# Narrow loads of the third tile: 768 columns instead of 1024, dealt anew over the DMA engines

## The chip, the cores and the metric

The kernel runs on one core of a Trainium2 chip. The metric is the device time of one execution in microseconds. The kernel before takes 2485.12 us (median of 3 runs, 2485.06 to 2485.26).

## The reference

A softmax with a temperature over the last axis of 16 x 256 rows of 32768 float32 numbers; the temperature is 1.0.

```python
scaled = logits / temperature
scaled = scaled - scaled.max(axis=-1, keepdims=True)
exp_scaled = np.exp(scaled)
return (exp_scaled / exp_scaled.sum(axis=-1, keepdims=True)).astype(np.float32)
```

512 MiB are read and 512 MiB written, and each number is read once and written once.

## The kernel before, in words

Each row of 32768 numbers is cut into two halves of 16384, so that the input is a matrix of 8192 half rows. 64 tiles of 128 half rows (8 MiB each) go one after the other through three slots of one large buffer in on-chip memory: tile g uses slot g modulo 3. Both halves of a row lie on neighbouring partitions of the same tile.

For each tile VectorE takes the maximum of three pieces of the half rows (L217), ScalarE makes the exponentials in place with the piece's own maximum and sums them (L277), and a few small instructions on both engines exchange the maxima and sums of neighbouring partitions and make one factor per piece (L235 to L262). ScalarE then scales the first piece (L296) and VectorE the two others (L268). The last two tiles have six smaller pieces. The instructions of VectorE and ScalarE stand in order: four tiles, a loop over three slots with 19 turns, and three tiles.

All transfers are issued by SyncE, in the order that `order` (L94) writes out by hand: loads of tiles 0, 1 and 2, store of tile 0, load of 3, stores of 1 and 2, and then load i, store i - 1 up to the end. A load (`load`, L137) waits until the store of the tile that was in its slot three tiles ago has landed (L145); a store (`store`, L156) waits until the tile is scaled (L162, L166). A plain load or store is one transfer of 128 rows of 64 KB, eight rows on each of the 16 DMA engines. Tile 0 is stored and tile 3 loaded in two halves, and the last tile is stored in three parts.

Tile 2 (`_SPLIT`) is the exception that the change is about. `load_parts` (L80) cuts it in a wide part and a narrow part of `_NARROW` columns at the end of the rows. The wide part is one transfer of 128 rows (L154). The narrow part is loaded in 19 transfers, each with the few rows of one list that `narrow_rows` (L69) makes from `_NARROW_ROWS`, the longest list first (L148 to L151):

```python
if g == _SPLIT and j == 1:
    for some in narrow_rows(P):
        sig.dma(
            key, nc.sync.dma_start(out=X[some, where], in_=x[rows, s : s + n][some])
        )
else:
    sig.dma(key, nc.sync.dma_start(out=X[:, where], in_=x[rows, s : s + n]))
```

A list of n rows takes every ninth row from its first one on. In the trace such a transfer of n rows puts one row on each of n DMA engines, the same first ones each time. So the lists set how many narrow rows each engine moves. The consumer waits for the wide part before its first piece and for all 19 narrow transfers before the piece that reaches into their columns (`landed`, L201).

Of the kernel before, what the change touches and what calls it, by code (L numbers as in the profile page):

```python
# [11 lines left out]
_LATE = ((4096, 3072, 3072, 2048, 2048, 2048), (3, 4, 5))  # L12
_LAST_STORES = ((0, 4096), (4096, 6144), (10240, 6144))
_SPLIT = 2
_NARROW = 1024
_NARROW_ROWS = (
    (13, 2), (12, 3), (14,), (11, 3), (10, 4), (9, 5), (8, 6), (7, 7), (4, 4, 3, 3),
)
_HEAD = 4
_TAIL = 3  # L20
# [329 lines left out]
```

## Time and profile before

| | before |
|---|---|
| median of 3 runs | 2485.12 us (2485.06 to 2485.26) |
| the profiled execution's own time | 2485.08 us |
| its span, first to last instruction | 2483.3 us |
| VectorE busy | 1526.0 us, 61% |
| ScalarE busy | 1325.5 us, 53% |
| DMA packets' time on the SyncE queue, share of 16 engines | 99.9% |
| data moved | 1073.78 MB, 432 GB/s over the span |

The span ends with SyncE's last wait for the stores. Between the span and the execution's time lie 1.8 us of launch and exit. The DMA share of a stretch counts a packet where it starts. The trace also keeps the start, the duration and the size of each DMA packet, but not on which of the 16 engines it ran.

### The profile page before, as it was taken

What the parts mean: (1) busy time and instruction counts of PE and PEld (TensorE: products, weight loads), DVE (VectorE), ACT (ScalarE), POOL (GpSimd) and SP (SyncE); (2) the same over time, 40 slices, a digit from 0 to 9 for tenths busy, and PEclk for the clock granted to TensorE, in tenths of its full rate; (3) what the DMA queues carried; (4) which work ended last, traced back from release to release, by engine and by line L of the source; (5) the groups of instructions that cost most, each with busy time, mean ns of one, the idle gap of its engine ahead of it and who ended that gap; (6) DMA issues with size and microseconds to landing.
All of it is one profiled execution on the core that took longest, in us unless ns stands there. A gap on an engine that the chain in (4) does not pass through costs nothing.

```text
span 2483.3 us, 1689 instructions
## 1 busy us (share of the span) xinstructions
DVE 1526.0 (61%) x776; ACT 1325.5 (53%) x529; POOL 0.2 (0%) x4
## 2 busy tenths in 40 slices
DVE  5845665666656656566565665656656666566665
ACT  4744654646546455464554645546455464554654
POOL 0000000000000000000000000000000000000000
DMA  9999999999999999999999999999999999999999
GB/s 409 438 433 438 431 432 438 432 435 432 434 436 429 436 436 433 432 438 433 430 436 435 434 434 435 437 429 437 435 432 434 437 436 430 436 436 431 435 436 391
DMA packets 19267, 1073.78 MB, mean 432 GB/s; under 512 B 2240, under 2 KB 2240, under 8 KB 2368
## 3 DMA queue, kind: packets, MB, share of 16 engines
q1 hardware_dynamic: 19264, 1073.75, 99.9%
q14 instruction: 3, 0.02, 0.0%
HBM read 536.87 MB, written 536.87 MB: 432 GB/s over the span
## 4 chain that ended last, share of the span: by engine, by line
DMA 61%; DVE 28%; ACT 7%; issue 2%; SPq 0%; DVEq 0%
DMA xs<-in_logits_dram 59%; DVE t L217 21%; ACT xs L277 6%; DVE xs L268 6%; DMA out_dram<-xs 3%; SPq L171 0%; ACT ee L288 0%; DVE junk L262 0%; DVE t L235 0%; ACT xs L296 0%; DVE row L259 0%; DVE row L239 0%; DVE junk L246 0%; DVEq L309 0%; DVEq L233 0%
## 5 line engine op out<-in xcount | busy, mean ns | idle before, releaser
L277 ACT ACTIVATE xs<-xs,t 128x6304 f32<-128x6304 f32 (+5 forms) x198 | 932.0, 4707 | 1052.1 <-DVE t L217 1045.3
L217 DVE TENSOR_REDUCE t<-xs 128x1 f32<-128x6304 f32 (+5 forms) x198 | 1110.0, 5662 | 617.0 <-DMA xs<-in_logits_dram 617.0
L296 ACT ACTIVATE xs<-xs,junk 128x6304 f32<-128x6304 f32 (+1 forms) x68 | 355.6, 5235 | 44.9 <-DVE junk L262 44.9
L268 DVE TENSOR_SCALAR xs<-xs,junk 128x5376 f32<-128x5376 f32 (+2 forms) x130 | 358.7, 2802 | 2.3
L235 DVE LOAD_MASK_SELECT t<-t x64 | 0.9, 14 | 282.9 <-ACT xs L277 282.9
L288 ACT ACTIVATE ee<-t,row 128x6 f32<-128x6 f32 (+1 forms) x64 | 19.2, 300 | 35.2 <-DVE row L239 35.2
L277 ACT ACTIVATION_READ_ACCUMULATOR xs<-xs,t 128x1 f32 x198 | 36.9, 186 | 0.0
L246 DVE CUSTOM_DVE_ANT_1 junk<-ee,t 128x6 f32<-128x6 f32 (+1 forms) x64 | 10.7, 167 | 23.5 <-ACT ee L288 23.5
L262 DVE TENSOR_SCALAR junk<-ee,row 128x3 f32<-128x3 f32 (+1 forms) x64 | 14.6, 228 | 2.2
L259 DVE RECIPROCAL row<-row 128x1 f32<-128x1 f32 x64 | 10.4, 163 | 2.2
L239 DVE TENSOR_REDUCE row<-t 128x1 f32<-128x6 f32 (+1 forms) x64 | 10.2, 159 | 2.2
L235 DVE STREAM_SHUFFLE t<-t 128x6 f32<-128x6 f32 (+1 forms) x64 | 10.4, 163 | 0.5
L246 DVE DVE_READ_ACCUMULATOR2_ANT row<- 128x1 f32 x64 | 5.3, 83 | 0.0
L277 ACT ACT_TABLE_LOAD x1 | 1.3, 1283 | 0.9 <-SPq L128 0.9
L331 POOL MEMSET const-bfloat16-1.0<- 128x1 bf16 x1 | 0.1, 102 | 0.0
L331 POOL MEMSET const-uint8-127<- 128x1 uint8 x1 | 0.1, 101 | 0.0
L331 POOL MEMSET const-float32-0.0<- 128x1 f32 x1 | 0.1, 99 | 0.2 <-issue 0.2
L331 POOL MEMSET const-float32-1.0<- 128x1 f32 x1 | 0.1, 98 | 0.0
## 6 DMA issues: line engine op xcount, KB each, us to landing
out_dram<-xs SPq DMA_DIRECT2D x2, 4096.0 KB, 26.9
xs<-in_logits_dram SPq DMA_DIRECT2D x2, 4096.0 KB, 19.4
xs<-in_logits_dram SPq DMA_DIRECT2D x1, 7680.0 KB, 59.7
out_dram<-xs SPq DMA_DIRECT2D x2, 3072.0 KB, 19.4
out_dram<-xs SPq DMA_DIRECT2D x1, 2048.0 KB, 12.2
xs<-in_logits_dram SPq DMA_DIRECT2D x62, 48.1
out_dram<-xs SPq DMA_DIRECT2D x62, 29.1
xs<-in_logits_dram SPq DMA_DIRECT2D x4, 12.0 KB
```

Of the source, the lines that this page charges most:

```text
L217: m = v.tensor_reduce(out=t[:, k : k + 1], in_=self.piece(k), axis=mybir.AxisListType.X, op=A.max, negate=True,)
L235: v.stream_shuffle(out=t[:, 2 * K : 4 * K], in_=t[:, 0 : 2 * K], mask=swap), "sh"
L239: v.tensor_reduce(out=r[:, 0:1], in_=tv[:, :, 0, :], axis=mybir.AxisListType.XY, op=A.min),
L246: v.tensor_tensor_reduce(out=f[:, 0 : 2 * K].rearrange("p (a k) -> p a k", a=2), in0=self.ev, in1=tv[:, :, 1, :], scale=1.0, scalar=0.0, o ...
L259: self.done(v.reciprocal(out=r[:, 2:3], in_=r[:, 1:2]), "rc")
L262: v.tensor_scalar_mul(out=f[:, 0:K], in0=e[:, 0:K], scalar1=r[:, 2:3]), "f"
L268: v.tensor_scalar_mul(out=xs, in0=xs, scalar1=f[:, k : k + 1]), k, self.p.own
L277: s = a.activation(out=xs, in_=xs, func=Exp, bias=t[:, k : k + 1], scale=inv_t, accum_out=t[:, K + k : K + k + 1],)
L288: a.activation(out=self.ev, in_=self.tv[:, :, 0, :], func=Exp, bias=r[:, 0:1], scale=-1.0),
L296: self.scaled(a.mul(out=xs, in_=xs, mul=f[:, k : k + 1]), k, self.p.on_act)
L331: nc = _bacc.Bacc("TRN2", target_bir_lowering=False, num_devices=1)
```

## The change

The narrow part of tile 2 becomes 768 columns wide instead of 1024, so the wide part grows from 15360 to 15616 columns, and the rows are dealt to other lists. There are 19 lists before and after.

```diff
-_NARROW = 1024
+_NARROW = 768
 _NARROW_ROWS = (
-    (13, 2), (12, 3), (14,), (11, 3), (10, 4), (9, 5), (8, 6), (7, 7), (4, 4, 3, 3),
+    (15,), (12, 3), (14,), (14,), (13, 1), (10, 4), (8, 6), (4, 4, 4, 2), (4, 4, 4, 2),
 )
```

Each group in round brackets deals the rows q, q + 9, q + 18 and so on of one remainder q, in order, to lists of the lengths given; one list has a single row after the change. On SyncE the 19 narrow transfers are issued from the same place, right behind the wide part's, and nothing else moves on any engine: the order of the instructions of VectorE, ScalarE and SyncE is the same but for the sizes of these 20 transfers.

## Prediction

> **What bounds the kernel now.** I read the page from the top: busy times, the DMA rows, the queue, and then the SyncE queue's timeline, because DMA came out as the bound.
>
> ```profile
> span 2483.3 us, 1689 instructions
> ...
> DVE 1526.0 (61%) x776; ACT 1325.5 (53%) x529; POOL 0.2 (0%) x4
> ...
> DMA  9999999999999999999999999999999999999999
> ...
> DMA packets 19267, 1073.78 MB, mean 432 GB/s; under 512 B 2240, under 2 KB 2240, under 8 KB 2368
> ...
> q1 hardware_dynamic: 19264, 1073.75, 99.9%
> ```
>
> VectorE has 39% of the span free and ScalarE 47%. The 16 DMA engines have nothing free: 99.9%. The chain of waits names VectorE and ScalarE too, but only because each store is issued after them; the engines meanwhile have other packets queued. The 2368 - 2240 = 128 packets between 2 and 8 KB are the narrow loads, one 4 KB packet per row.
>
> The trace keeps every packet's start, duration and size. An engine starts its next packet 3 to 4 ns before the modelled end of the last, so the packets can be threaded into 16 chains. I number the chains by how many 4 KB packets they hold: 19, 19, 18, 14, 11, 10, 9, 7, 6, 5, 4, 3, 2, 1, 0, 0. That is exactly "a transfer of n rows puts one row on each of the first n engines". No chain has a gap over 0.75 us, so an engine's last packet ends at its start plus its own work plus what its packets lose to contention. The slowest engine sets the end. The DMA share in stretches at the end shows how unequal they are:
>
> ```profile
> 2476.00:2476.50 0.50, 0.00 (x0) 0.00 (x0) 0.00 (x0) 1.00 0.69 295
> 2476.50:2477.50 1.00, 0.00 (x0) 0.00 (x0) 0.00 (x0) 1.00 0.68 295
> 2477.50:2479.00 1.50, 0.00 (x0) 0.00 (x0) 0.00 (x0) 1.00 0.53 229
> 2479.00:2480.50 1.50, 0.00 (x0) 0.00 (x0) 0.00 (x0) 1.00 0.19 82
> 2480.50:2482.00 1.50, 0.00 (x0) 0.00 (x0) 0.00 (x0) 1.00 0.04 16
> ```
>
> The last two columns are DMA share and GB/s. Engines drop out from 2476.0 on; engines 11 to 15 end at 2476.0 to 2476.3, engines 0 to 3 at 2480.6 to 2480.8, and engine 4 last of all at 2481.60 us. From there to the profiled time of 2485.08 us are 3.48 us of completion and exit, which I keep. The profiled run is 0.04 us under the median of 2485.12 us, so the sum holds for both.
>
> **The change, part by part.**
>
> Issue. The 19 narrow issues of SyncE stay 19.
>
> ```profile
> 0.95 1.32 SPq L154 DMA_DIRECT2D xs<-in_logits_dram  x3
> 2.31 13.89 SPq L151 DMA_DIRECT2D xs<-in_logits_dram  x19
> 51.70 0.84 SPq L171 DMA_DIRECT2D out_dram<-xs  x2
> ```
>
> They are done at 16.2 us; the engines reach them at about 58 us. Cost nothing, hidden by 42 us of queued tiles. Behind them waits only the first store, issued at 51.70 after ScalarE, not after them.
>
> Landing. Tile 2's reduce starts at 80.19 us and its last third, the only one that reads narrow columns, near 92 us, while the narrow packets end before 64 us. Cost nothing; cover 28 us.
>
> Work of each engine. Packets outside contention: 64 KB 2418 ns, 60 KB 2267, 32 KB 1213, 16 KB 611, 4 KB 159; so 37.65 ns per KB. The wide load's eight packets grow from 60 to 61 KB: +301 ns on every engine. A narrow packet shrinks to 3 KB, 121.4 ns; with its 9 ns completion packet and two overlaps of 3.6 ns, one narrow load costs an engine 161.2 ns before and 123.6 after. With the new counts (row lists read the same way) each engine's work changes by 301 + 123.6 x new - 161.2 x old:
>
> ```
> engine      0    1    2    3    4    5    6    7    8    9   10   11   12   13   14   15
> old count  19   19   18   14   11   10    9    7    6    5    4    3    2    1    0    0
> new count  19   18   16   15    8    8    7    7    6    6    5    5    4    3    1    0
> change ns -413 -537 -623 -102 -483 -322 -284  +38  +75 +237 +275 +435 +473 +511 +425 +301
> ```
>
> By this alone engine 4 ends at 2481.60 - 0.48 = 2481.12, engine 3 at 2480.66, and the time is 2481.12 + 3.48 = **2484.6 us**.
>
> What the Trainium skill says of a row list with one row in it. The trace of before has no one-row transfer; its smallest, two rows, went to two engines. "DMA: Bandwidth & Descriptors", section "Why a DMA increments its semaphore by 16 and not by 1", says the count of engines is the largest number up to 16 that divides the slowest dimension that is not 1; for one row that would be the 768 columns, so 16 packets of 192 B. By this rule engine 0 loses one 123.6 ns load and all engines gain a packet, an estimate of some 20 ns each by the rows' 9 ns completion packet; the sum would be 2484.6 still.
>
> Losses at the narrow loads themselves. Around 57 to 61 us the last wide packet took 0.2 to 1.2 us too long on 14 engines, and six of the 128 narrow ones 0.5 to 0.8 us instead of 0.16, where some engines are in their narrow loads and others still in the wide one; engine 0 stood 0.74 us. A narrow row need not go to the engine that writes its partition in a wide load, so two engines may be writing where one did. As many narrow loads start among the same wide packets after the change, with other partners. I take the same losses; bounds are none of them (about 1 us off every engine) and half as much again (0.5 us more).
>
> Contention later on. This is the term with most freedom, since the order in which engines run is what the change moves. In the trace almost every packet that is long after 64 us is the last of a load's eight: 113 of 123 that are over by 15 ns or more. An engine that is behind reads its last packet while those ahead already store, and loses 30 to 550 ns there. That pushes it further back, until it no longer meets them; from 1250 us on all engines but number 4 take 2418 ns a packet, with three or four exceptions. Lags behind the first engine, at its first store and at the end: engines 0 to 3 from 2.3-3.1 to 4.6-4.7 us; engines 5, 6 and 8 from 1.1-1.3 to 3.2-3.5; engines 7, 9 and 10 from 0.6-0.8 to 1.3-1.7; engines 11 to 15 stay under 0.45. Engine 4 goes from 1.57 to 5.56; of this 2.0 us are a trickle of its own, 0.2 us in each 250 us, to the end.
>
> After the change the lags at the first store are (old start plus change): engines 0 to 3 at 2.2, 2.1, 1.9 and 1.7 us, and twelve engines within 0.7 us, number 4 at 0.58. The first engine ends 0.5 us later, at 2476.55. Bounds: with no push, engines 0 to 3 end at 2476.55 + 2.2 = 2478.75 and engine 4 at 2476.55 + 0.58 + 2.0 = 2479.1, time 2482.6; with the old spread formed again, 2476.55 + 5.56 = 2482.1, time 2485.6. I take the old push for the four: 2.2 + 1.5 = 3.7, end 2480.25, time 2483.7. Engine 4 with the push of its new nearest neighbour by lag (old engine 10, 0.60 to 1.31: 0.7) ends at 2479.8, with its own old push of 4.0 at 2481.1, time 2484.6. Between 2483.7 and 2484.6, **2484.1 us**.
>
> A measurement of this kernel can tell about 0.2%, 5 us, from no change; so 2480.1 to 2490.1 counts as the same.
>
> **The rivals.**
>
> 1. *The old spread forms again* (slower than before, 0.5 us). Twelve engines in 0.7 us are a crowd where five stood; if no more than some five can stay together, the rest is pushed back group by group and drives engines 0 to 3 ahead of it. For it: the gaps of 0.8 to 1.6 us between the groups at the end of before. Against it: engines under 0.8 us behind lost next to nothing until 800 us. It decides where the pushes add up to over 3 us: 2485.6 us, up to 2487 with the engine-4 trickle falling on the last group.
> 2. *No push.* The twelve lie below the 0.8 us at which losses began, and engines 0 to 3 have only one group ahead of them, over 1 us clear. Against it: engine 4 was at 1.57 and was pushed. 2482.6 us.
> 3. *The losses do not die out* (slower). Place: the last packet of each load on engines 0 to 3, with twelve engines storing at once. Price: engine 8 lost 2.0 us from 200 to 1000 us, that is 97 ns at each of some 20.7 loads; over 62 loads 6.0 us, so 2478.75 + 6.0 + 3.48 = 2488.2; at its worst stretch (1.02 us from 600 to 800 us) 12 us, 2494. It passes "slower" from 130 ns a load on. Against it: in before every group came free by 1250 us. Beside it stands "DMA: Bandwidth & Descriptors", section "Latency and other measured facts", row on HBM row pitch: lock-stepped streams from rows a large power of two apart fell from 207 to 164 and 103 GB/s. Its pitches begin at 512 KiB and here rows lie 64 KiB apart; the trace speaks against a loss of that kind, since between 7.4 and 50 us all 16 engines ran within 1.1 us of each other and no 64 KB packet took over 2444 ns.
> 4. *It does not do what it says:* the trace has no one-row transfer, and the new one might be split over all 16 engines in place of one. Then engine 0 has one load of 123.6 ns less and every engine a small packet more, which by the 9 ns packets and the 37.65 ns per KB is some 25 ns with its completion. It moves no case by more than 0.15 us (3 in 10, inside the others).
>
> **How the numbers follow.** Forecast 2483 to 2485: 0.47. Rival 1, 2485 to 2487: 0.27. Rival 2, 2482 to 2483: 0.17. Rival 3: 0.08, half of it over 2490.1. Left, 0.01, for a gain over 0.2%: the mean of all 16 ends is 2478.5, which with perfect balance would give 2482.0, so only a loss of contention on top of that could do it. Range 2482.0 to 2487.0. Faster 0.01, same 0.95, slower 0.04.
>
> **What would show it.** Wide load 7808 KB, and 3 KB packets of some 121 ns: the work term. The DMA share falling from 2476.5 on instead of 2476.0, and one late group near 2480: the forecast; an engine ending at 2482: rival 1; all over by 2479.2: rival 2; long last packets still there past 1250 us: rival 3; packets under 512 B above 2240: rival 4. Wrong altogether if an engine runs dry: the tightest place is the last tile's first store, issued 1.29 us before the first engine starts it; a first engine later by 0.5 us only widens that.

## Result, and the profile after

The changed kernel takes 2507.82 us (median of 20 runs, 2485.31 to 2511.45), against 2485.15 us before (20 runs, 2484.68 to 2486.06). The ratio of the mean times is 1.0071, 95% interval 1.0053 to 1.009 (of the medians 1.0091): slower, and outside the forecast of 2482 to 2487 us. The runs of before lie within 1.4 us. Those of the changed kernel fall in two groups: four of 20 at 2485.3 to 2488.2 us, near the forecast, and sixteen at 2496.6 to 2511.5. The profiled one took 2496.59 us, with a span of 2494.8 us.

The page of the changed kernel, the lines that answer to those of before:

```profile
span 2494.8 us, 1689 instructions
...
DVE 1526.2 (61%) x776; ACT 1325.5 (53%) x529; POOL 0.2 (0%) x4
...
DMA  9999999999999999999999999999999999999998
...
DMA packets 19267, 1073.78 MB, mean 430 GB/s; under 512 B 2240, under 2 KB 2240, under 8 KB 2368
...
q1 hardware_dynamic: 19264, 1073.75, 99.8%
```

The same work, and still 99.8% of 16 engines busy: the page hardly shows the loss, because a packet that takes longer counts as busy for longer. That no packet under 512 B was added says that the one-row load was not split. The end, by stretches (last columns DMA share and GB/s):

```profile
2486.00:2487.00 1.00, 0.00 (x0) 0.00 (x0) 0.00 (x0) 1.00 0.41 172
2487.00:2488.50 1.50, 0.00 (x0) 0.00 (x0) 0.00 (x0) 1.00 0.27 115
2488.50:2490.00 1.50, 0.00 (x0) 0.00 (x0) 0.00 (x0) 1.00 0.30 131
2490.00:2491.50 1.50, 0.00 (x0) 0.00 (x0) 0.00 (x0) 1.00 0.30 131
2491.50:2493.50 2.00, 0.00 (x0) 0.00 (x0) 0.00 (x0) 1.00 0.09 37
```

From 2487 us on only some five engines of sixteen work. By the threaded packets eleven end at 2486.7 to 2486.9 us, one at 2490.6, and engines 0 to 3 at 2492.4 to 2493.2. So both moved: the first end by 10.7 us (2476.0 before) and the distance from first to last end from 5.6 to 6.5 us. The issues at the start are as they were:

```profile
0.96 1.33 SPq L154 DMA_DIRECT2D xs<-in_logits_dram  x3
2.33 13.24 SPq L151 DMA_DIRECT2D xs<-in_logits_dram  x19
51.63 0.85 SPq L171 DMA_DIRECT2D out_dram<-xs  x2
```

Where the time went is told by equal stretches of the middle, here of the changed kernel:

```profile
310.00:620.00 310.00, 190.73 (x96) 165.32 (x64) 0.00 (x0) 1.00 1.00 435
620.00:930.00 310.00, 190.73 (x96) 165.32 (x64) 0.00 (x0) 1.00 1.00 433
930.00:1240.00 310.00, 190.74 (x96) 165.31 (x64) 0.00 (x0) 1.00 1.00 434
1240.00:1550.00 310.00, 190.74 (x96) 165.31 (x64) 0.00 (x0) 1.00 1.00 435
1550.00:1860.00 310.00, 190.74 (x96) 165.33 (x64) 0.00 (x0) 1.00 1.00 433
1860.00:2170.00 310.00, 189.93 (x96) 164.58 (x64) 0.00 (x0) 1.00 1.00 427
```

Before has 433 to 435 GB/s in each of them, and in the last:

```profile
1860.00:2170.00 310.00, 190.70 (x96) 165.31 (x64) 0.00 (x0) 1.00 1.00 434
```

Until about 1800 us the kernel is nearly as fast as before: its store at 1778.86 us is 2.9 us later than the same one of before. Then it drops to 427 GB/s with 100% DMA share. SyncE's queue in that part, a store and the next load at each tile:

```profile
1974.50 0.33 SPq L171 DMA_DIRECT2D out_dram<-xs  x1
1974.87 0.43 SPq L154 DMA_DIRECT2D xs<-in_logits_dram  x1
2014.27 0.33 SPq L171 DMA_DIRECT2D out_dram<-xs  x1
2014.64 0.43 SPq L154 DMA_DIRECT2D xs<-in_logits_dram  x1
2053.30 0.33 SPq L171 DMA_DIRECT2D out_dram<-xs  x1
```

and the same stretch of before:

```profile
1969.31 0.33 SPq L171 DMA_DIRECT2D out_dram<-xs  x1
...
2007.98 0.33 SPq L171 DMA_DIRECT2D out_dram<-xs  x1
...
2046.66 0.33 SPq L171 DMA_DIRECT2D out_dram<-xs  x1
```

In these lines tiles follow each other every 38.67 us before, and after 39.8 and 39.0 us. From 1779 us on the mean is 39.2, that is 0.55 us more for each tile. The waits (us in total, times, longest), of before and then of the changed kernel, say who waited:

```profile
DVE t L217 <- DMA xs<-in_logits_dram: 617.0, 60, 23.5
```

```profile
DVE t L217 <- DMA xs<-in_logits_dram: 627.7, 60, 23.4
```

VectorE waited 617.0 us for loads before and 627.7 after: compute is not longer, loads land later.

Why, is seen from two numbers of each store, read from the landings of a transfer on its 16 engines. **Spread** is the time from the first engine's landing to the last one's. **Lead** is the time from the store's issue to its first engine's landing less the 19.35 us that an engine's eight packets of a tile take; it shows how long before its turn the store was issued. Near 385, 850, 1310, 1780 and 2240 us:

```
lead / spread, us     385         850         1310        1780        2240
before                6.03/3.68   5.06/4.66   4.98/4.71   4.84/4.92   4.41/5.36
after                 6.02/4.30   4.20/5.75   3.52/6.20   2.14/8.60   2.00/7.83
```

Lead and spread add up to 9.7 to 10.3 us until the lead is gone: two transfers take 2 x 19.35 = 38.7 us, and from the last engine's landing of a load to the issue of its store go 29 us of compute (in the changed kernel's timeline from VectorE's start at 1985.38 to the issue at 2014.27 us: 28.9). What is left, 9.7 us, is shared by spread and lead. The lead hardly falls under 2.0 us (1.90 is the lowest in this trace). The first load of before, which finds all engines free, has the same: issued at 0.95 us, it first lands at 22.33, and less 19.35 that leaves 2.03 us. So that is what an issue and a completion take. Once the spread passes 7.7 us, which is 9.7 less 2.0, the leading engines can get no further ahead: their next store hangs on the load that engines 0 to 3 land last, with 29 us of compute in between. Whatever engines 0 to 3 lose from then on, all lose.

The packets bear this out, and show what it does not explain. A 64 KB packet takes 2418 ns where nothing delays it. From 1000 to 1250 us the 64 KB packets of all 16 engines of the changed kernel together take 1.9 us longer than that, all of it on the five engines that trail. From 2000 to 2250 us it is 50.0 us, some 3 us on every engine, and the engines together stand without a packet for 3.8 us (0.4 in the earlier stretch). That is 3.3 us for each engine in 6.4 tiles, 0.52 us a tile, close to the 0.55 above. So all engines now go at one pace. But the leading ones are hardly seen to stand idle; they lose most of their time in last packets of stores. And the trailing ones lose 2.9 to 3.3 us each where they had lost 0.3 to 0.6. The loop says why all 16 share the loss; why it is some 0.5 us a tile is open.

### The profile page after: what moved, and what is told of

It is laid out like the page before. It is cut to its first block, busy times and chain, and to the rows that moved or that the text cites. A ratio compares the mean times of both kernels' runs of the same rounds, so it can differ in the third digit from the quotient of the medians.

```text
span 2494.8 us, 1689 instructions
## 1 busy us (share of the span) xinstructions
DVE 1526.2 (61%) x776; ACT 1325.5 (53%) x529; POOL 0.2 (0%) x4
## 2 busy tenths in 40 slices
DMA packets 19267, 1073.78 MB, mean 430 GB/s; under 512 B 2240, under 2 KB 2240, under 8 KB 2368
## 3 DMA queue, kind: packets, MB, share of 16 engines
q1 hardware_dynamic: 19264, 1073.75, 99.8%
## 4 chain that ended last, share of the span: by engine, by line
DMA 62%; DVE 28%; ACT 7%; issue 2%; SPq 0%; DVEq 0%
DMA xs<-in_logits_dram 59%; DVE t L217 21%; ACT xs L277 6%; DVE xs L268 6%; DMA out_dram<-xs 3%; SPq L171 0%; ACT ee L288 0%; DVE junk L262 0%; DVE t L235 0%; DVE row L259 0%; ACT xs L296 0%; DVE row L239 0%; DVE junk L246 0%; DVEq L309 0%; DVEq L233 0%
## 5 line engine op out<-in xcount | busy, mean ns | idle before, releaser
L217 DVE TENSOR_REDUCE t<-xs 128x1 f32<-128x6304 f32 (+5 forms) x198 | 1110.0, 5663 | 627.7 <-DMA xs<-in_logits_dram 627.7
L246 DVE CUSTOM_DVE_ANT_1 junk<-ee,t 128x6 f32<-128x6 f32 (+1 forms) x64 | 10.7, 167 | 23.5 <-ACT ee L288 23.5
```

The source lines that it names most:

```text
L217: m = v.tensor_reduce(out=t[:, k : k + 1], in_=self.piece(k), axis=mybir.AxisListType.X, op=A.max, negate=True,)
L246: v.tensor_tensor_reduce(out=f[:, 0 : 2 * K].rearrange("p (a k) -> p a k", a=2), in0=self.ev, in1=tv[:, :, 1, :], scale=1.0, scalar=0.0, o ...
```

## The experiments

Theory A: engines 0 to 3 are pushed back at their loads' last packets, cannot get clear of the pack of twelve, and eat up the lead; the time is then lost because stores are issued too late. Theory B, the rival: the packets just take longer the further engines fall behind; the lead plays no part. Each run names the median of its runs; before took 2485.04 to 2485.15 us beside them.

**after_half**: the changed kernel with more lead.

```diff
-                    in_=self.piece(k),
+                    in_=self.piece(k)[:, : self.p.pieces[k][1] // (2 if self.p.looped else 1)],
```

> The changed kernel, but in the 57 tiles of the loop VectorE takes the maximum over the first half of each piece alone (the other columns are left out of the maximum; the exponentials and sums still cover all). That shortens the way from a load's landing to the store's issue by 3.4 us (the first piece's maximum from 6.6 to 3.3 us; ScalarE sets the rest). Theory A (the issue comes too late): four engines fall back until the store that hangs on the slowest landing is issued less than 1 us before the leading engines need it; with 3.4 us more, that lead starts near 10 us instead of 6.8 and stays over 1 us; median under 2492 us, no long last packets of stores. Theory B (contention alone grows with the lag): the lead plays no part; 2495 to 2511 us as the changed kernel.

2486.67 us (10 runs, 2486.04 to 2489.74; ratio to before 1.0008, interval 0.9998 to 1.0018). The same stretches:

```profile
1240.00:1550.00 310.00, 122.45 (x96) 163.56 (x64) 0.00 (x0) 1.00 1.00 435
1550.00:1860.00 310.00, 122.44 (x96) 163.56 (x64) 0.00 (x0) 1.00 1.00 434
1860.00:2170.00 310.00, 122.45 (x96) 163.55 (x64) 0.00 (x0) 1.00 1.00 435
```

No drop. The engines fell back at first even more than in the changed kernel: spread 4.66, 6.90, 6.91, 6.81, 6.96 us at the five times above. There it stops, with a lead of 6.4 us, and from 2000 to 2250 us the 64 KB packets of all engines together lose 0.4 us, against 50.0. Nearly the whole loss is gone, though the spread is larger than ever in before. That is theory A against B. The run also halves what VectorE reads for its maximum, so alone it does not part the lead from that reading; before_half and late_tiny_2us below bear on it.

**lists_1024** and **width_768**: one half of the change each.

```diff
 _NARROW = 1024
-    (13, 2), (12, 3), (14,), (11, 3), (10, 4), (9, 5), (8, 6), (7, 7), (4, 4, 3, 3),
+    (15,), (12, 3), (14,), (14,), (13, 1), (10, 4), (8, 6), (4, 4, 4, 2), (4, 4, 4, 2),
```

> The new row lists with the old width of 1024 columns. Theory A, with the four engines behind a close pack of twelve as the cause of the steady falling back: as slow as the changed kernel or more, 2495 to 2512 us, since the four now start 2.8 us behind instead of 2.4. If the width of 768 is the cause: 2484 to 2487 us as before.

2498.74 us (10 runs, 2485.02 to 2507.99; ratio 1.004, 1.0016 to 1.0063). Four of ten runs at 2485.0 to 2486.3, six at 2497 to 2508: the lists alone give both groups. In its trace the lead is 3.49 at 1314 and 2.19 us at 1781, the spread 6.55 and 8.95.

```diff
-_NARROW = 1024
+_NARROW = 768
```

> The old row lists with the new width of 768 columns. Theory A with the dealing as the cause: near before, 2483 to 2488 us, as the engines are still spread step by step, over three quarters of the distance. If the width is the cause: 2495 to 2512 us.

2485.42 us (10 runs, 2484.97 to 2486.36). The width does no harm; spread 4.35 us at 1312.

**plain**: no narrow loads.

```diff
-    if g == _SPLIT:
-        return [(0, _W - _NARROW), (_W - _NARROW, _NARROW)]
```

> No narrow loads: tile 2 is loaded in one transfer. All engines then start the first store within about 1 us of each other. If engines under 0.8 us apart do not disturb each other (the twelve of the changed kernel lost nothing until 1700 us), they stay together and the time is the earliest ends of before plus the lag of the last, 2480.5 to 2483.5 us. If engines that are close by disturb each other the more, 2490 to 2515 us.

2487.12 us (10 runs, 2486.05 to 2488.29; ratio 1.0008, 0.9998 to 1.0018). Neither: they don't stay together (spread 3.7 at 385, 3.9 at 850 us) and the lead never falls under 5.4. The interval holds 1, but every run lies above every one of the 31 runs of before beside it, so the narrow part seems to bring before some 2 us. My picture that engines under 0.8 us apart leave each other alone holds for eleven of the twelve in the changed kernel, not for sixteen.

**graded**: the four as in the changed kernel, the pack pulled apart.

```diff
-    (15,), (12, 3), (14,), (14,), (13, 1), (10, 4), (8, 6), (4, 4, 4, 2), (4, 4, 4, 2),
+    (12, 3), (11, 4), (14,), (10, 4), (9, 5), (8, 6), (8, 6), (7, 7), (9, 2, 2, 1),
```

> 768 columns, engines 0 to 3 with the 19, 18, 16 and 15 narrow loads of the changed kernel, but the other twelve spread out: 13, 12, 10, 8, 6, 4, 3, 2, 1, 1, 0, 0 in place of 8, 8, 7, 7, 6, 6, 5, 5, 4, 3, 1, 0. If the pack of twelve is what the four can't get clear of: 2484 to 2488 us, spread of the landings under 5.5 us. If the count of the four alone is the cause: 2495 to 2512 us.

2485.26 us (10 runs, 2484.97 to 2485.68). Spread 5.05 us at 849, 1313 and 1776 us, at rest until then (5.5 at the end), and a lead of 4.67. So it is the pack that engines 0 to 3 do not get clear of, not their own count.

**steps**: distances of the end of before from the start.

```diff
-_NARROW = 1024
+_NARROW = 1664
-    (13, 2), (12, 3), (14,), (11, 3), (10, 4), (9, 5), (8, 6), (7, 7), (4, 4, 3, 3),
+    (11, 4), (11, 4), (11, 3), (11, 3), (11, 3), (8, 6), (8, 6), (8, 6), (8, 6),
```

> Groups of engines set apart from the start at about the distances at which the kernel before ends up: 1664 columns, 18 lists, counts 18, 18, 18, 15, 13, 13, 9, 9, 5, 5, 5, 0, 0, 0, 0, 0, at 256 ns each, so 4.6, 3.3, 2.3, 1.3 and 0 us. If engines lose only until they are clear of each other, they lose little here, and the end is their mean without losses (some 2477.3) plus 10 loads of 256 ns plus 3.48: 2483.4 us, 2483 to 2485. If the distances of before are not what keeps them clear: 2486 us or more.

2484.64 us (10 runs, 2484.41 to 2485.12); 0.4 us under before's 2485.05 and under the changed kernel in every run. The interval of the ratio, 0.9988 to 1.0007, holds 1, so a gain over before is not shown. The spread is 5.26 us at 345 us, rests there until 1000 us and grows to 6.5 us by 2320: set-apart groups lose little at first, but they pay for the distance at the end.

**before_half**: control for the shorter maximum, the edit of after_half in the kernel before.

> The kernel before with the shorter maximum of the run after_half (half of each piece's columns left out of the maximum in the tiles of the loop). Theory A: before never ran out of lead, its stores being issued 5 us ahead, so 3.4 us more bring nothing: 2484.5 to 2486 us. If the compute bounds before in some other way, it gets faster by over 1 us.

2485.70 us (10 runs, 2485.46 to 2486.24). More lead (8.4 us at 845) brings before nothing. The spread grows as in before or more (6.17 us at 2237, before 5.36), so reading less does not keep the engines together.

**before_late**: the kernel before with less lead.

```diff
             self.wait(v, "rc")
+            if self.p.looped:
+                v.tensor_reduce(
+                    out=r[:, 3:4],
+                    in_=self.piece(2)[:, :3800],
+                    axis=mybir.AxisListType.X,
+                    op=A.max,
+                )
```

> The kernel before with one more instruction of VectorE in each of the 57 tiles of the loop, a maximum over 3800 columns of the third piece into an unused number, ahead of the factors; by the 6.7 us of 6304 columns it takes 4.0 us, and each store is issued that much later. Theory A (the issue comes too late): the first engine then reaches a store 6.0 - 4.0 = 2 us after its issue at 345 us and 1 us or less from about 900 us on, where some 1 us is what an issue needs anyway; so the kernel slows like the changed one though its row lists are the old ones: 2493 to 2515 us. Theory B (contention alone grows with the lag): the lags are those of before and so is the time, 2484 to 2487 us.

2516.34 us (4 runs, 2513.47 to 2518.6; ratio 1.0125, 1.0108 to 1.0142). The added line and the stretches:

```profile
456.31 4.11 DVE L262 TENSOR_REDUCE row<-xs 128x1 f32<-128x3800 f32 x1
```

```profile
310.00:620.00 310.00, 219.74 (x104) 162.17 (x65) 0.00 (x0) 1.00 1.00 431
620.00:930.00 310.00, 219.01 (x103) 162.97 (x64) 0.00 (x0) 1.00 1.00 427
```

The lead is 2.12 us at 388 and 2.02 at 858: at its floor from the start, with a spread of only 3.7 to 4.8 us. Old row lists, no wide spread, and yet 31 us slower, 39.2 us a tile: with the lead gone, the kernel before slows as the changed one does. The added maximum also reads 3800 columns more; the runs from late_tiny on part the two.

**after_split** and **before_split**: more lead with nothing left out, the loop's loads in two halves each.

```diff
-    if g == 3:
+    if 3 <= g < 61:
...
-                    value = 16 if j == 1 else self.p.n16
+                    value = 16 if j == 1 and not self.p.looped else self.p.n16
```

> The changed kernel with the loads of the loop's 57 tiles in two halves, as tile 3 is loaded; the first piece's maximum then starts before the second half lands, and the way from the last landing to the store's issue gets 7 us shorter with nothing left out. The halves cost each engine eight packets of 1213 in place of half as many of 2418 ns and one completion more, some 70 ns a tile, 4.0 us in all. Theory A: the lead stays over the floor of 2 us, so 2486.7 (as with the shortened maximum) + 4.0: 2489 to 2493 us. Theory B: 2499 to 2515 us.

> The kernel before with the same halves: before never ran out of lead, so only the price of the halves shows, 2485.1 + 4.0: 2488 to 2490.5 us. It is the control for after_split.

2490.18 us (10 runs, 2489.98 to 2490.94) and 2490.68 us (10 runs, 2490.53 to 2490.88). With halves the two row lists give the same. The price was 5.5 us for the control, not 4.0. It is no clean test of the lead: in after_split the spread stayed at 3.3 to 3.7 us until 1307 us (6.2 in the changed kernel), so the halves also kept the engines from falling back. In before_split they did not: 4.76 us at 1307, as in before (4.71).

**after_again**: a second trace of the changed kernel.

> The changed kernel once more, for a second trace. Theory A: up to the tile at which the lead reaches its floor of 2 us the tiles follow each other every 38.65 us, from there on every 39.2; so the time is near 2485 us + 0.55 us for each tile after that point (the first trace: at 1800 us, 2496.6 us; a time of 2510 us would have the point near 700 us). Theory B: the tiles get longer step by step, with no such point.

2509.59 us (4 runs, 2506.03 to 2512.59), the profiled one 2511.12. Its stretches:

```profile
310.00:620.00 310.00, 190.73 (x96) 165.32 (x64) 0.00 (x0) 1.00 1.00 434
620.00:930.00 310.00, 189.88 (x96) 164.52 (x64) 0.00 (x0) 1.00 1.00 432
930.00:1240.00 310.00, 185.93 (x95) 160.57 (x64) 0.00 (x0) 1.00 1.00 427
```

The lead is gone by 853 us in place of some 1740. Lead and spread: 5.01/4.71 at 385, 2.00/7.68 at 853, 2.01/8.01 at 1794. From 853 us to the end are (2480 - 853) / 39.2 = 41.5 tiles at 0.55 us: 22.8 us. With the 4 lost up to 853 that is 26.8, against 26.0 us of span over before. So in both traces the time is set by when the lead runs out. The two groups of runs fit that, if in the quick ones (four of 24) it does not run out; no trace of a quick run of this kernel was taken.

**before_late_2us**: half the delay, `[:, :1900]` in place of `[:, :3800]`.

> The kernel before with an added maximum over 1900 columns in place of 3800, 2.0 us a tile. Theory A: the lead of before (6.0 us at 345 us, 4.4 at 2279) falls to 4.0 and 2.4, still over the floor of 2.0, so nothing shows: 2484.8 to 2486.5 us. If every delay of an issue costs time, half of what the 4 us cost: 2495 to 2505 us.

2508.16 us (4 runs, 2507.07 to 2509.26; ratio 1.0094, 1.0077 to 1.0111). **Theory A as I had put it missed here.** The lead was 3.94 us at 386, as worked out, but the spread then did not follow that of before: 5.53 us at 852 (before 4.66) and 6.12 at 1321, the lead 2.18 and 2.02. Either a later issue makes engines fall back more, or the added reading does. Three runs were to tell:

```diff
+            if self.p.looped:
+                for i in range(12):
+                    v.reciprocal(out=D[self.p.slot][:, i : i + 1], in_=r[:, 1:2])
```

> The kernel before with twelve more reciprocals of one column ahead of the factors in each tile of the loop; at 0.16 us each they put the issue of the store off by 2.0 us, as the maximum over 1900 columns did (2508 us), but read next to nothing. If the later issue itself makes the engines fall back faster: 2495 to 2510 us, spread growing past 5 us by 900 us. If VectorE's extra reading did it: 2484.8 to 2486.5 us.

2484.96 us (10 runs, 2484.75 to 2485.35). The dose was wrong: pipelined, twelve reciprocals took 0.83 us, not 2.0.

```profile
455.52 0.83 DVE L264 RECIPROCAL d<-row 128x1 f32<-128x1 f32 x12
```

```diff
+    Z = nc.alloc_sbuf_tensor("z", [P, 1900], fp32)
...
+            if self.p.looped:
+                v.tensor_reduce(
+                    out=r[:, 3:4], in_=Z[:, :], axis=mybir.AxisListType.X, op=A.max
+                )
             self.wait(v, "sum")
```

> The kernel before with a maximum over 1900 columns of a separate buffer in each tile of the loop, where VectorE waits 4.4 us for ScalarE's sums anyway, so that no store is issued later. If VectorE's extra reading makes the engines fall back: 2495 to 2510 us. If the later issue does: 2484.8 to 2486.5 us.

2485.24 us (10 runs, 2485.09 to 2486.11). Reading as much without a later issue does no harm in time; the spread is larger than in before, though, 5.47 us at 849.

> The shortened maximum of before_half (half of each piece's columns left out of the maximum in the loop) together with the 1900-column delay of before_late_2us: the issue stands 1.4 us earlier than before in spite of the added instruction. If only the lead counts: it stays over 5 us, 2485 to 2487 us. If the added instruction does harm by itself: 2495 us or more.

2485.83 us (10 runs, 2485.55 to 2486.17); lead 6.5 us, spread 4.8 at 847 us. The same instruction is harmless where there is lead, with the maximum halved as in before_half. Then the delay without reading at the right dose:

> Thirty small reciprocals in place of twelve. In late_tiny twelve of them took 0.83 us, not 2.0, so that run was too small a dose; thirty take 2.0 to 2.1 us, as the 1900-column maximum did. If the later issue itself makes the engines fall back until the lead is gone: 2495 to 2510 us. If a delay without reading of this size is harmless: 2484.8 to 2486.5 us.

> Eighteen small reciprocals, 1.2 us. If the harm sets in step by step with the delay: between late_tiny (2485.0 us at 0.8) and the run above. If it needs the lead to run down near its floor: 2484.8 to 2486.5 us.

Thirty reciprocals, 1.92 us: 2486.01 us (10 runs, 2485.17 to 2509.75; ratio 1.003, 1.0006 to 1.0054), six runs at 2485.2 to 2486.1 and four at 2491.0, 2502.2, 2502.8 and 2509.8. Its trace is of a quick run (2485.39 us; lead 3.75, spread 4.13 at 850), and there the lead does not run out: it is still 3.12 us at 2319. Eighteen, 1.19 us: 2485.06 us (10 runs, 2484.93 to 2485.68).

```profile
455.52 1.92 DVE L264 RECIPROCAL d<-row 128x1 f32<-128x1 f32 x30
```

The 19 runs of before beside them end at 2485.91 us. So a later issue alone, with next to nothing more to read, can tip the kernel, with 1.9 us in four runs of ten and with 0.8 or 1.2 us in none. That the maximum over 1900 columns tipped all four is not explained by the delay alone; it took 2.13 us and read the tile as well. Whether a shrinking lead speeds up the falling back, or extra reading adds to the spread, stays open.

## Why the prediction was wrong, point by point

1. *What bounds the kernel: the slowest engine's own work.* Right for before. The sentence that failed stands there too: compute is on the chain "only because each store is issued after them; the engines meanwhile have other packets queued". That cover has a size, 9.7 us less the spread, of which 2.0 us are needed for an issue and a completion. I put what happens when it is used up at nothing, without a reason; it cost 0.55 us a tile from then on.
2. *Issue and landing of the narrow loads: nothing.* Right: 13.24 us of issue, tile 2 not held up.
3. *Work of each engine.* Right in size. The trace has 3 KB packets at 121 ns and 61 KB ones at 2305 (worked out 121.4 and 2304.7). At their first store engines 0 to 3 lag by 2.5, 2.4, 2.3 and 2.1 us (forecast 2.2, 2.1, 1.9, 1.7), all twelve others within 0.64 (0.7).
4. *The one-row load.* It went to one engine: there are 128 packets of 3 KB for 128 rows, and the count of small packets stayed 2240. My reading of the Trainium skill, "DMA: Bandwidth & Descriptors", section "Why a DMA increments its semaphore by 16 and not by 1", that the row would be split in 16, is not borne out. The section goes by the sizes as the instruction carries them, and the trace has this transfer as 1 x 1 elements of 3072 B.
5. *Contention.* This is the term that was mis-sized: "I take the old push for the four: 2.2 + 1.5 = 3.7". They lag by 6.4 to 6.7 us at the store issued at 1585 us, because a pack of twelve lay ahead of them, as graded showed. The price a load I had under rival 3 (97 ns) was near: engine 0 lost 4.2 us from 200 to 1750 us, 104 ns at each of 40 loads. But I added it to those engines alone and had it end by itself. By itself the larger push would have cost little: after_half has a spread of 7.0 us and takes 2486.67 us, still in my range. What made 11 to 26 us of it is the step under 1, that no store would be issued too late: the push used up the lead.
6. *Rival 3* had the place, and with 2488 to 2494 us came nearest, at 0.08; the median lies 14 us above it, and the mechanism behind the larger times was not in it. Its engines were to be late for themselves; in truth they made all engines late. Of the loss by row pitch that stands beside it there is no sign: eleven of the twelve in the pack, in step within 0.7 us, lost under 0.2 us from 100 to 1750 us.
7. *"Wrong altogether if an engine runs dry".* It came to that in effect: the leading engines ran up against the issue of every store, though little of it shows as idle time (3.8 us over 16 engines from 2000 to 2250 us). I looked for the tightest issue in the trace of before, the last tile's first store, and saw that it widens. I should have asked which issues tighten when the spread grows: every store of the loop.

## What to carry to other kernels

Where transfers are queued ahead of a compute step, work out the lead: the time of the transfers in between, less the compute from the last landing to the issue, less the spread of the engines; of this some 2 us are needed here for an issue and a completion. The DMA share stays at 100% while that lead shrinks, and a change that shifts load between engines uses it up; ask what it is at the end of the run, not at the start. A kernel whose runs fall in two groups may be near such a threshold, so look at many runs and not at one median.

## What the runs showed of the hardware

- DMA engines that share a stream lost 30 to 550 ns in before, and up to 650 in the changed kernel while it had lead, at the last of a load's eight packets when others already store, and so drifted apart over tens of tiles: from 3.1 to 5.6 us in before, to 7.0 us at rest in after_half. Which part of the chip they contend for, no run here shows.
- Two halves in place of one 64 KB row kept the engines of the changed kernel together, within 3.7 us until 1307 us; those of before drifted apart in spite of them, to 4.76 us.
- With the lead gone, in the changed kernel the leading engines' time is lost mostly in a packet that is not the first: of the losses from 2000 to 2250 us, summed over the twelve engines (one of them, the one that ends at 2490.6, trails too), some 31 us stand on the last packets of stores, 2.9 us on those of loads, and 2.6 us on first packets. Why the last packet of a store takes longer there is open.
- Small VectorE instructions on one column run closer together than their single duration says: 0.16 us alone, 0.07 in a row of twelve.
